# A fused layer in fp32 halves: the inverse's masks moved from GpSimd to the products' way out of PSUM, the first MLP products in source order, and the last stores issued behind the next loads

## The chip, the cores and the metric

One core of a Trainium2 chip runs the whole program. The metric is the device time of one execution in microseconds, median of several runs. Engines are named as in the profile: PE (TensorE matmul), PEld (its weight loads), DVE (VectorE), ACT (ScalarE), POOL (GpSimd), and SP, whose queue issues all the DMAs of this kernel.

## The reference, cut to what matters

One layer on x of 1024 tokens x 1024 channels (DEPTH is 1):

```python
u = rms_norm(h, norm_mix); proj = u @ w_in                      # 1024 x 2568
pool_out = pool_mixer(proj[:, :512], w_pool, pool_scale)        # 4 groups, trailing means of 2, 4, 8, 16 frames
qkv = causal_conv_silu(proj[:, 512:2048], conv_w)
gdn_out = gated_delta_net(q, k, v, z, a, b, ...)                # 4 heads of 128; solves (I + M) X = R, M strictly lower
h = h + concat(pool_out, gdn_out) @ w_out
u = rms_norm(h, norm_mlp)
h = h + square(relu(u @ w_up)) @ w_down                         # w_up 1024 x 4096, w_down 4096 x 1024
out = rms_norm(h, norm_final)
```

The kernel takes the delta rule in chunks of 128 tokens. In each chunk and head it needs the inverse of a unit lower triangular 128 x 128 matrix.

## The kernel before, in words

Every large product is made of three fp32r matmuls: an operand is split into a rounded part ("hi", a cast by ACT) and the rest ("lo", a subtraction by DVE or POOL), and hi x hi, hi x lo and lo x hi are added up in one PSUM bank (`mm3`).

**Order of the work.** PE's order is written out by hand: the whole program stands in `tc.manual_schedule(engines={PE})`, and in the first half a virtual clock (`T.now`) interleaves the dense projections with eight strands of small work. The other engines and SP are ordered by the planner of the framework, which plays the program through with its own costs. The planner also gives tiles their slots. `issue_after(ins)` puts what follows behind `ins` in the queue of its engine.

**Projection and delta rule (about 60 to 480 us of the span).** Dense projections run with `prepare`, `query`, `invert`, `correct` and `scan` between them, once for each of 8 chunks, for 4 heads at a time (tiles of 128 x 512). `invert` doubles the size of the inverted blocks seven times. Level 0 masks the matrix `m1` with `lev[0]` on DVE (L578) and adds the identity (L579). In each of the levels 1 to 6, POOL makes `bl = m1 * lev[l]` (L588), PE makes `px = bl^T t`, DVE takes it out of PSUM as `xx = px + ident` (L592), and PE makes the two products of the next level. The seven masks are made once on POOL at the start (L255 to L260: two memsets and two selects each). POOL also has the subtractions of `split_w` (L133) for half of the projections, and smaller steps.

**MLP, up (about 515 to 843 us).** One step of Strassen's scheme with seven products: `w_up` is taken in 16 pairs of 128-column blocks (`wu`, 1 MB each), and product i of pair p is 4 x 3 matmuls with the token operand `TH[i], TL[i]`. Pairs 0 and 1 run side by side in the order 1, 2, 6, 5, 3, 7, 4, because the operands for the second half of the tokens are made only now: `turn_second` transposes the normed tokens into 8 banks, makes the rows R11, R12, R2 from the banks (L908, L925) and splits operands 6 and 3; `operands_5`, `operands_7`, `operands_4` make the others (`parts_of`: L912 on ACT, L913 on DVE); `operands_7` also makes R4 = R21 - R2 on DVE (L943). `up_ready` prepares a weight operand: sums within `wu` (L970, L972, L975, L982; on DVE for pairs 0 and 1, on POOL for the others) and a split (L954 ACT, L955 DVE). `get_ready` runs `up_ready` two products ahead. `norm_v(1, 1)` norms the last two token tiles.

**MLP, down (from about 846 us).** Hidden values go through DRAM (`hd`): `keep` stores them at once (L994), but those of the last pair, but for product 1, are put on the list `late`. `down_load` fetches a block of `w_down` (L1103) and one of hidden values (L1106), four steps ahead, and the list `late` is stored after the first four. The pools of these tiles (`wr`, `xr`, `nf`, opened in this order) lie on the memory of the up stage's operands, tile by tile (`reuse_waits="tile"`): a load starts when the up operand under its slot has had its last matmul.

Of the kernel before, what the change touches and what calls it, by code (L numbers as in the profile page):

```python
# [8 lines left out]
F32 = mybir.dt.float32  # L9
F32R = mybir.dt.float32r  # L10
# [18 lines left out]
def hybrid_trunk(ctx, tc, x, norm_mix, w_in, conv_w, w_pool, pool_scale, a_log, dt_bias,  # L29
# [218 lines left out]

    lev = []
    for l in range(7):  # L250
        b = 1 << l
        m = gp.tile([P, P], F16, name=f"lev{l}")
        nb = P // (2 * b)
        m3 = m.rearrange("p (n q) -> p n q", q=2 * b)
        G.memset(m3[:, :, 0:b], 0.0)  # L255
        G.memset(m3[:, :, b:2 * b], -1.0)

        G.affine_select(m3, m3, pattern=[[-2 * b, nb], [0, 2 * b]], compare_op=ALU.is_ge, fill=0.0, base=0,
                        channel_multiplier=1)
        G.affine_select(m3, m3, pattern=[[2 * b, nb], [0, 2 * b]], compare_op=ALU.is_gt, fill=0.0, base=b,  # L260
                        channel_multiplier=-1)
        lev.append(m)
# [310 lines left out]
    def invert(c, r):  # L573

        m1 = r["m1"]
        t, tt = gt("t", 3, F16), gt("tt", 3, F16)
        b0 = gt("bl", 2, F16)
        V.tensor_tensor(b0, m1, bc(lev[0]), op=ALU.mult)  # L578
        V.tensor_tensor(tt, b0, bc(ident_h), op=ALU.add)  # L579
        yield 1.0 * SLACK  # L580
        pt = bank()
        for h in range(NH):
            T.matmul(pt[:, h, :], tt[:, h, :], ident_h, start=True, stop=True)
        A.copy(t, pt)
        yield 0.9 * SLACK
        for l in range(1, 7):
            bl = gt("bl", 2, F16)
            G.tensor_tensor(bl, m1, bc(lev[l]), op=ALU.mult)  # L588
            px = bank()
            mm(px, bl, t)  # L590
            xx = gt("xx", dt=F16)
            V.tensor_tensor(xx, px, bc(ident), op=ALU.add)  # L592
            yield 1.0 * SLACK
            pt, ptt = bank(), bank()
            mm(pt, tt, xx)
            mm(ptt, xx, tt)
            t, tt = gt("t", 3, F16), gt("tt", 3, F16)
            A.copy(t, pt)
            A.copy(tt, ptt)
            if l < 6:  # L600
                yield 1.0 * SLACK
        r.update(t=t, tt=tt)
        done(f"inverted{c}", 1.0 * SLACK)
# [279 lines left out]
    ys += norm_v(1, 1)  # L883
# [5 lines left out]
    R[12], R[2] = (u3(f"r{n}", F32) for n in (12, 2))  # L889
    TH[3], TL[3], TH[6], TL[6] = (u3(nm, F32R) for nm in ("th3", "tl3", "th6", "tl6"))  # L890

# [26 lines left out]
    def turn_second(ys):  # L918

        for k in range(KT):  # L920
            pt = turned_banks[k] = acc_bank() if k in (0, 1, 6, 7) else work_bank()
            turn(ys, k, pt)
            j = k % 4
            if k < 4:
                A.activation(R[12][:, j, :], pt, AF.Copy, scale=nmlp[:, k:k + 1])  # L925
                weighed(R[11][:, j, :], k, R[11][:, j, :])
            else:
                weighed(R[2][:, j, :], k, R[11][:, j, :])
        parts_of(6, rows_of(2))
        for j in range(4):  # L930
            weigh(turned_banks[4 + j], 4 + j, TH[3][:, j, :], TL[3][:, j, :], nmlp)

    def operands_5():
        TH[5], TL[5] = (big_tile(f"t{m}5", [4, HALF], F32R) for m in "hl")
        parts_of(5, rows_of(11))

    def operands_7():

        for j in range(4):
            weighed(R[12][:, j, :], 4 + j, R[12][:, j, :])  # L940
        R[4] = [c_tile("r4") for _ in range(4)]
        for j in range(4):
            V.tensor_tensor(R[4][j], R[21][:, j, :], R[2][:, j, :], op=ALU.subtract)  # L943
        TH[7], TL[7] = u3("th7", F32R), big_tile("tl7", [4, HALF], F32R)
        parts_of(7, rows_of(12))
# [17 lines left out]

    def up_ready(p, i):
# [3 lines left out]
        eng = V if p < 2 else G  # L968
# [7 lines left out]
        if i == 1 and p < 2:  # L976
            out = split(src, [P, 4, P], cp, "c", "c", 9)
        else:
            out = split(src, [P, 4, P], ws, "wh", "wl", 5)
        made2.add((p, i))  # L980
        if i in (2, 6) and {(p, 2), (p, 6)} <= made2:
            eng.tensor_tensor(a12, a12, a11, op=ALU.subtract)  # L982
        return out

    late = []

# [27 lines left out]
    def up_product(p, i, w):  # L1014
# [27 lines left out]
        else:  # L1042
# [5 lines left out]
    order = [(0, 1), (1, 1), lambda: turn_second(ys), (0, 2), (1, 2), operands_5, (0, 6), (1, 6), operands_7,  # L1048
             (0, 5), (1, 5), (0, 3), (1, 3), operands_4, (0, 7), (1, 7), (0, 4), (1, 4)]
# [20 lines left out]
    used = 0  # L1070
    for e in order:
        if callable(e):
            e()
            continue
# [8 lines left out]

    wrc, wr = opened(name="wr", bufs=4, side="right", reuse_waits="tile")
    xrc, xr = opened(name="xr", bufs=4, side="right", reuse_waits="tile")
    nfc, nf = opened(name="nf", bufs=1, side="right", reuse_waits="tile")
# [8 lines left out]
    def down_load(i, s):  # L1095
# [10 lines left out]
        nc.sync.dma_start(out=x, in_=hd[s][i])  # L1106
# [61 lines left out]
    for n, (i, s) in enumerate(todo):  # L1168
# [3 lines left out]
        while late:  # L1172
            store(*late.pop(0))
# [16 lines left out]
    close(spc)  # L1190
    close(nfc)
    close(xrc)
    close(wrc)
# [30 lines left out]
```

## Time and profile before

| | us |
|---|---|
| runs (3): median, lowest, highest | 1162.3, 1160.35, 1165.93 |
| the profiled execution: its own time | 1163.48 |
| its span | 1161.8 |
| PE busy | 1100.9 |
| DVE busy | 789.8 |
| ACT busy | 601.5 |
| POOL busy | 303.5 |

The profiled execution is 1.2 us above the median of the runs, and its span leaves 1.7 us of its own time outside. The granted clock of PE was 0.987 of full speed over the span. PE is "busy" also while it runs at half clock, so its busy time is not all work at full speed.

### The profile page before, as it was taken

What the parts mean: (1) busy time and instruction counts of PE and PEld (TensorE: products, weight loads), DVE (VectorE), ACT (ScalarE), POOL (GpSimd) and SP (SyncE); (2) the same over time, 40 slices, a digit from 0 to 9 for tenths busy, and PEclk for the clock granted to TensorE, in tenths of its full rate; (3) what the DMA queues carried; (4) which work ended last, traced back from release to release, by engine and by line L of the source; (5) the groups of instructions that cost most, each with busy time, mean ns of one, the idle gap of its engine ahead of it and who ended that gap; (6) DMA issues with size and microseconds to landing.
All of it is one profiled execution on the core that took longest, in us unless ns stands there. A gap on an engine that the chain in (4) does not pass through costs nothing.

```text
span 1161.8 us, 15593 instructions
## 1 busy us (share of the span) xinstructions
PE 1100.9 (95%) x5606; PEld 893.6 (77%) x5606; DVE 789.8 (68%) x1240; ACT 601.5 (52%) x1113; POOL 303.5 (26%) x272
## 2 busy tenths in 40 slices
PE   6998999988998999997999999999989999999997
PEld 5776777767776787876788888888878888888886
DVE  5798688867879775669655555555465687466584
ACT  6666566564755555546554544454444334335353
POOL 6033365564755422000232313131100000000010
PEclk9999999998999999998999999999989999999999
DMA  5233121111223321120634343444298796265561
GB/s 161 82 98 121 56 59 41 55 52 40 55 60 118 109 65 55 37 73 18 209 133 166 128 162 137 156 144 146 89 373 298 270 393 224 94 199 194 186 215 73
DMA packets 93049, 155.24 MB, mean 134 GB/s; under 512 B 7782, under 2 KB 45739, under 8 KB 92971
## 3 DMA queue, kind: packets, MB, share of 16 engines
q1 hardware_dynamic: 92970, 154.24, 39.4%
q8 instruction: 44, 0.72, 0.3%
q14 instruction: 35, 0.28, 0.1%
HBM read 120.66 MB, written 33.55 MB: 133 GB/s over the span
## 4 chain that ended last, share of the span: by engine, by line
PE 70%; DVE 13%; ACT 3%; issue 2%; POOL 1%; DMA 1%; POOLq 0%; DVEq 0%; ACTq 0%
PE bank L44 52%; PE acc L44 18%; DVE cy L391 2%; DVE nxt L410 1%; DVE xx L592 1%; PE bank L48 1%; DVE wl L955 1%; DVE nxt L409 0%; DMA wu<-in_w_up_dram 0%; DVE r L908 0%; DVE tl L913 0%; ACT th L172 0%; DVE ul L173 0%; DMA raw<-in_w_out_dram 0%; DVE kn L533 0%
## 5 line engine op out<-in xcount | busy, mean ns | idle before, releaser
L44 PE MATMUL bank<-tl,wh 128*128 128x512 f32 x440 | 175.3, 398 | 5.8 <-DVE tl L913 5.8
L44 PE MATMUL bank<-th,wh 128*128 128x512 f32 x440 | 175.2, 398 | 0.3 <-ACT p L1024 0.3
L44 PE MATMUL bank<-th,wl 128*128 128x512 f32 x440 | 174.7, 397 | 0.0
L954 ACT CAST sh<-x 128x1024 fp32r<-128x1024 f32 x55 | 57.9, 1053 | 163.8 <-PE bank L44 155.1
L954 ACT CAST wh<-wu 128x512 fp32r<-128x512 f32 x110 | 68.0, 620 | 127.2 <-PE bank L44 120.7
L44 PE MATMUL bank<-th,sh 128*128 128x512 f32 x344 | 133.8, 389 | 0.0
L44 PE MATMUL bank<-th,sl 128*128 128x512 f32 x344 | 133.8, 389 | 0.0
L44 PE MATMUL bank<-tl,sh 128*128 128x512 f32 x344 | 133.8, 389 | 0.0
L44 PE MATMUL acc<-uh,wh 128*128 128x512 f32 x320 | 130.3, 407 | 1.6 <-DVE ul L173 0.9
L44 PE MATMUL acc<-ul,wh 128*128 128x512 f32 x320 | 129.3, 404 | 0.0
L44 PE MATMUL acc<-uh,wl 128*128 128x512 f32 x320 | 128.9, 403 | 0.0
L955 DVE TENSOR_TENSOR sl<-x,sh 128x1024 fp32r<-128x1024 f32 x55 | 67.3, 1224 | 89.5 <-ACT sh L954 89.4
L44 PEld LDWEIGHTS bank<-tl,wh 128*128 128x128 f32 x440 | 83.5, 190 | 26.8 <-DVE tl L913 7.8
L955 DVE TENSOR_TENSOR wl<-wu,wh 128x512 fp32r<-128x512 f32 x110 | 84.4, 768 | 28.4 <-ACT wh L954 26.8
L44 PEld LDWEIGHTS bank<-th,wh 128*128 128x128 f32 x440 | 83.3, 189 | 20.1 <-ACT p L1024 0.8
L44 PEld LDWEIGHTS bank<-th,wl 128*128 128x128 f32 x440 | 83.5, 190 | 19.3
L152 POOL TENSOR_TENSOR stf<-stf,mhalf 128x1 f32<-128x1 f32 x8 | 7.9, 998 | 327.3 <-DVE stf L1159 327.3
L588 POOL TENSOR_TENSOR bl<-m,lev 128x512 f16<-128x512 f16 x48 | 62.9, 1310 | 84.7 <-PE bank L44 72.3
L391 DVE SCALAR_TENSOR_TENSOR cy<-cr,cols,cy 128x512 f32<-128x512 f32 x72 | 73.2, 1022 | 9.0 <-ACT cy L389 8.4
L133 POOL TENSOR_TENSOR wl<-raw,wh 128x512 fp32r<-128x512 f32 x48 | 68.0, 1420 | 35.6 <-ACT wh L132 35.4
L44 PEld LDWEIGHTS bank<-th,sl 128*128 128x128 f32 x344 | 64.6, 188 | 13.5
L44 PEld LDWEIGHTS bank<-th,sh 128*128 128x128 f32 x344 | 64.5, 188 | 13.5
(336 smaller groups left out, 2365.4 us busy)
## 6 DMA issues: line engine op xcount, KB each, us to landing
w<-in_w_down_dram SPq DMA_DIRECT2D x72, 512.0 KB, 5.9
x<-hd SPq DMA_DIRECT2D x56, 512.0 KB, 3.5
raw<-in_w_in_dram SPq DMA_DIRECT2D x80, 256.0 KB, 2.7
wu<-in_w_up_dram SPq DMA_DIRECT2D x16, 1024.0 KB, 5.3
hd<-s SPq DMA_DIRECT2D x48, 256.0 KB, 2.3
raw<-in_w_out_dram SPq DMA_DIRECT2D x24, 256.0 KB, 2.7
xin<-in_x_dram SPq DMA_DIRECT2D x8, 512.0 KB, 5.3
h<-in_x_dram SPq DMA_DIRECT2D x8, 512.0 KB, 4.4
```

The lines of the kernel that those rows point to most:

```text
L44: T0.matmul(out, lhsT, rhs, start=start, stop=stop, skip_group_check=goes_on)
L48: T0.transpose(out, in_, identity)
L133: eng.tensor_tensor(lo, raw, hi.bitcast(F32), op=ALU.subtract)
L152: last["rsqrt"] = G.tensor_tensor(s, s, mhalf[:, :n], op=ALU.pow)
L391: V.scalar_tensor_tensor(cy, cr[:, e:e + HALF], tap[e], cy, op0=ALU.mult, op1=ALU.add)
L410: V.tensor_tensor(nxt[:, n:], cur[:, n:], cur[:, :W - n], op=ALU.add)
L588: G.tensor_tensor(bl, m1, bc(lev[l]), op=ALU.mult)
L592: V.tensor_tensor(xx, px, bc(ident), op=ALU.add)
L954: A.copy(hi, src)
L955: V.tensor_tensor(lo, src, hi.bitcast(F32), op=ALU.subtract)
```

## The change

Three parts. (1) `invert` multiplies with the full `m1` and puts the mask on the product as DVE takes it out of PSUM: `xx = px * lev[l]`, with masks that are turned round and have ones on the diagonal; POOL's 48 masking steps go, and level 0 is one DVE step in place of two. The masks take one select more each. (2) For the first 14 up products PE, DVE and ACT run in source order; operand 5 is made ahead of 6 and its product goes ahead; R4 and two of the weight sums move from DVE to POOL; the first block of `w_up` of pairs 0 and 1 gets loads of its own (`first_load`, 256 KB each) ahead of `norm_v(1, 1)`. (3) The late stores are issued behind the last of the first loads of the down stage, and the pools are opened in another order (`nf`, `xr`, `wr`).

```diff
@@ masks
-        G.memset(m3[:, :, 0:b], 0.0)
-        G.memset(m3[:, :, b:2 * b], -1.0)
...
+        first = l > 0
+        G.memset(m3[:, :, 0:b], -1.0 if first else 0.0)
+        G.memset(m3[:, :, b:2 * b], 0.0 if first else -1.0)
...
+        G.affine_select(m, m, pattern=[[-1, P]], compare_op=ALU.not_equal, fill=1.0, base=0, channel_multiplier=1)
@@ invert
-        b0 = gt("bl", 2, F16)
-        V.tensor_tensor(b0, m1, bc(lev[0]), op=ALU.mult)
-        V.tensor_tensor(tt, b0, bc(ident_h), op=ALU.add)
+        V.tensor_tensor(tt, m1, bc(lev[0]), op=ALU.mult)
...
-            bl = gt("bl", 2, F16)
-            G.tensor_tensor(bl, m1, bc(lev[l]), op=ALU.mult)
             px = bank()
-            mm(px, bl, t)
+            mm(px, m1, t)
             xx = gt("xx", dt=F16)
-            V.tensor_tensor(xx, px, bc(ident), op=ALU.add)
+            V.tensor_tensor(xx, px, bc(lev[l]), op=ALU.mult)
@@ operands of the up products
-    ys += norm_v(1, 1)
...
-    R[12], R[2] = (u3(f"r{n}", F32) for n in (12, 2))
     TH[3], TL[3], TH[6], TL[6] = (u3(nm, F32R) for nm in ("th3", "tl3", "th6", "tl6"))
+    R[2], R[12] = (u3(f"r{n}", F32) for n in (2, 12))
...
     def turn_second(ys):
+        TH[5], TL[5] = (big_tile(f"t{m}5", [4, HALF], F32R) for m in "hl")
         for k in range(KT):
             pt = turned_banks[k] = acc_bank() if k in (0, 1, 6, 7) else work_bank()
             turn(ys, k, pt)
...
+        for k in range(4):
+            A.activation(R[12][:, k, :], turned_banks[k], AF.Copy, scale=nmlp[:, k:k + 1])
+            weighed(R[11][:, k, :], k, R[11][:, k, :])
+        parts_of(5, rows_of(11))
+        for j in range(4):
+            weighed(R[2][:, j, :], 4 + j, R[11][:, j, :])
         parts_of(6, rows_of(2))
+
+    def operands_3():
+        R[4] = [c_tile("r4") for _ in range(4)]
         for j in range(4):
+            G.tensor_tensor(R[4][j], R[21][:, j, :], R[2][:, j, :], op=ALU.subtract)
             weigh(turned_banks[4 + j], 4 + j, TH[3][:, j, :], TL[3][:, j, :], nmlp)
...
     def operands_7():
...
-        R[4] = [c_tile("r4") for _ in range(4)]
-        for j in range(4):
-            V.tensor_tensor(R[4][j], R[21][:, j, :], R[2][:, j, :], op=ALU.subtract)
@@ weights of the up products
+    def first_load(p):
+        r = ws.tile([P, 4, P], F32, name="raw", tag="raw", bufs=3)
+        nc.sync.dma_start(out=r, in_=wuv[:, :4, p * 256:p * 256 + P])
+        return split(r, [P, 4, P], cp, "c", "c", 9)
...
-        eng = V if p < 2 else G
+        eng = V if p < 2 and i in (1, 6) else G
...
         if i == 1 and p < 2:
-            out = split(src, [P, 4, P], cp, "c", "c", 9)
+            out = first_parts[p]
...
+        eng = G
         if i in (2, 6) and {(p, 2), (p, 6)} <= made2:
             eng.tensor_tensor(a12, a12, a11, op=ALU.subtract)
...
+    first_parts = [first_load(p) for p in range(2)]
+    ys += norm_v(1, 1)
@@ order
-    order = [(0, 1), (1, 1), lambda: turn_second(ys), (0, 2), (1, 2), operands_5, (0, 6), (1, 6), operands_7,
-             (0, 5), (1, 5), (0, 3), (1, 3), operands_4, (0, 7), (1, 7), (0, 4), (1, 4)]
+    order = [(0, 1), (1, 1), lambda: turn_second(ys), (0, 2), (1, 2), operands_3, (0, 5), (1, 5), operands_7, (0, 6), (1, 6),
+             (0, 3), (1, 3), operands_4, (0, 7), (1, 7), (0, 4), (1, 4)]
+    N_FIRST = 14
...
+        if e == (0, 1):
+            get_ready(3)
+            in_order.enter_context(tc.manual_schedule(engines={mybir.EngineType.PE, mybir.EngineType.DVE, mybir.EngineType.Activation}))
+        elif used == N_FIRST:
+            in_order.close()
         if callable(e):
+            get_ready(used + 2 + LEAD)
             e()
@@ down
+    nfc, nf = opened(name="nf", bufs=1, side="right", reuse_waits="tile")
+    xrc, xr = opened(name="xr", bufs=4, side="right", reuse_waits="tile")
     wrc, wr = opened(name="wr", bufs=4, side="right", reuse_waits="tile")
-    xrc, xr = opened(name="xr", bufs=4, side="right", reuse_waits="tile")
-    nfc, nf = opened(name="nf", bufs=1, side="right", reuse_waits="tile")
...
-        nc.sync.dma_start(out=x, in_=hd[s][i])
+        last["load"] = nc.sync.dma_start(out=x, in_=hd[s][i])
...
-        while late:
-            store(*late.pop(0))
+        if late:
+            with tc.issue_after(last["load"].ins):
+                while late:
+                    store(*late.pop(0))
```

## Rows read from the trace of the kernel before

**Rows 1.** The page's busy time, share of the span and count of each engine.
```profile
PE 1100.9 (95%) x5606; PEld 893.6 (77%) x5606; DVE 789.8 (68%) x1240; ACT 601.5 (52%) x1113; POOL 303.5 (26%) x272
```

**Rows 2.** Busy time by stage. Columns: the stretch, its length, busy time (and count) of PE, PEld, DVE, ACT, POOL, then PE's mean granted clock, the DMA share and GB/s.
```profile
60.00:480.00 420.00, 390.34 (x2503) 316.95 (x2502) 326.37 (x607) 246.53 (x568) 197.64 (x151) 0.98 0.22 67
...
515.00:560.00 45.00, 37.20 (x163) 28.55 (x162) 40.59 (x66) 26.06 (x48) 1.34 (x2) 0.92 0.14 48
560.00:840.00 280.00, 279.67 (x1203) 226.48 (x1202) 158.29 (x230) 139.09 (x230) 72.72 (x56) 1.00 0.41 145
840.00:860.00 20.00, 16.76 (x61) 12.81 (x60) 13.72 (x16) 10.86 (x14) 0.00 (x0) 0.83 0.97 341
```

**Rows 3.** What PE waited for from 60 to 480 us: us in total, times, the longest.
```profile
PE bank L44 <- DVE xx L592: 15.3, 10, 3.0
PE bank L48 <- DVE kn L533: 2.9, 2, 1.5
```

**Rows 4.** What PE waited for from 440 us to the end, same columns.
```profile
PE bank L44 <- DVE tl L913: 5.8, 3, 5.3
PE bank L44 <- ACT wh L954: 3.2, 1, 3.2
PE bank L44 <- DVE c L955: 1.7, 2, 1.5
```

**Rows 5.** POOL's groups over the whole span: count, then busy us and mean ns of one, then idle time before them and its releasers.
```profile
L588 POOL TENSOR_TENSOR bl<-m,lev 128x512 f16<-128x512 f16 x48 | 62.9, 1310 | 84.7 <-PE bank L44 72.3 <-DVE tt L579 7.2 <-DVE m L550 3.6
...
L258 POOL TENSOR_SCALAR_AFFINE_SELECT lev<-lev 128x128 f16<-128x128 f16 x7 | 2.9, 416 | 0.0
```

**Rows 6.** DVE's groups from 60 to 440 us, same columns.
```profile
L391 DVE SCALAR_TENSOR_TENSOR cy<-cr,cols,cy 128x512 f32<-128x512 f32 x56 | 60.0, 1076 | 7.5 <-ACT cy L389 7.0
L592 DVE TENSOR_TENSOR xx<-bank,ident 128x512 f16<-128x512 f32 x45 | 30.7, 683 | 14.5 <-PE bank L44 14.4
...
L764 DVE TENSOR_TENSOR ml<-pT,mh 128x512 fp32r<-128x512 f32 x8 | 8.4, 1058 | 0.0
L393 DVE SCALAR_TENSOR_TENSOR vT<-vT,cy 128x512 f32<-128x512 f32 x8 | 8.0, 995 | 1.8 <-ACT vT L392 1.8
...
L578 DVE TENSOR_TENSOR bl<-m,lev 128x512 f16<-128x512 f16 x8 | 6.5, 809 | 0.1
...
L619 DVE TENSOR_TENSOR hh<-bank,tt 128x512 f16<-128x512 f32 x7 | 4.8, 681 | 0.2 <-PE bank L44 0.2
```

**Rows 7.** Durations of single lines, ns min/median/max: the convolution's taps from 60 to 440 us, `xx` and the split of `pT` over the span.
```profile
L391 DVE SCALAR_TENSOR_TENSOR cy<-cr,cols,cy x56: 736/752/1833, 59.8 to 315.8; 128x512 f32<-128x512 f32 x56
...
L592 DVE TENSOR_TENSOR xx<-bank,ident x48: 671/682/693, 89.1 to 452.7; 128x512 f16<-128x512 f32 x48
...
L764 DVE TENSOR_TENSOR ml<-pT,mh x16: 678/682/1777, 369.0 to 504.8; 128x512 fp32r<-128x512 f32 x16
```

**Rows 8.** PE's instructions in order of time from 515 to 545 us: start, us, engine, line, operation, out<-in, count, and in brackets the idle time before.
```profile
522.81 1.04 PE L48 MATMUL acc<-ident,xn 128*128 128x128 f32 x8
...
526.95 0.48 PE L44 MATMUL bank<-th,wh 128*128 128x512 f32 x1
527.26 0.39 PE L44 MATMUL bank<-tl,wh 128*128 128x512 f32 x1
527.49 0.40 PE L44 MATMUL bank<-th,wl 128*128 128x512 f32 x1
...
540.34 0.80 PE L44 MATMUL bank<-tl,wh 128*128 128x512 f32 x1 [5.27 <-DVE tl L913]
540.93 0.63 PE L44 MATMUL bank<-th,wl 128*128 128x512 f32 x1
541.36 0.63 PE L44 MATMUL bank<-th,wh 128*128 128x512 f32 x1
```

**Rows 9.** DVE in the same stretch, in order of time, same columns.
```profile
526.40 2.72 DVE L908 SCALAR_TENSOR_TENSOR r<-bank,cols,r 128x512 f32<-128x512 f32 x4
...
537.19 2.49 DVE L943 TENSOR_TENSOR r<-r,r 128x512 f32<-128x512 f32 x4
```

**Rows 10.** Durations of single lines from 500 to 575 us, ns min/median/max: the splits of `wu` on DVE, and a weight sum on POOL.
```profile
L955 DVE TENSOR_TENSOR wl<-wu,wh x18: 679/683/1283, 515.8 to 574.5; 128x512 fp32r<-128x512 f32 x18
...
L970 POOL TENSOR_TENSOR wu<-wu x2: 1296/1300/1304, 559.5 to 562.8; 128x512 f32<-128x512 f32 x2
```

**Rows 11.** SP's issues around 840 us in order of time.
```profile
839.81 0.32 SPq L994 DMA_DIRECT2D hd<-v  x1
840.22 0.39 SPq L1103 DMA_DIRECT2D w<-in_w_down_dram  x1
840.66 0.50 SPq L1106 DMA_DIRECT2D x<-hd  x1
843.35 0.38 SPq L1103 DMA_DIRECT2D w<-in_w_down_dram  x1
```

**Rows 12.** ACT around 845 us in order of time.
```profile
844.75 0.63 ACT L998 ACTIVATE p<-p 128x512 f32<-128x512 f32 x1
845.35 0.62 ACT L954 CAST wh<-x 128x512 fp32r<-128x512 f32 x1
```

**Rows 13.** PE from 842 to 853 us in order of time.
```profile
846.54 0.79 PE L44 MATMUL bank<-wh 128*128 128x512 f32 x1 [3.22 <-ACT wh L954]
...
852.22 0.48 PE L44 MATMUL bank<-wh 128*128 128x512 f32 x1
```

More of the change, by code (lines that the diff above doesn't have):

```diff
@@ L254, in hybrid_trunk @@
         m3 = m.rearrange("p (n q) -> p n q", q=2 * b)
-        G.memset(m3[:, :, 0:b], 0.0)
-        G.memset(m3[:, :, b:2 * b], -1.0)
-        G.affine_select(m3, m3, pattern=[[-2 * b, nb], [0, 2 * b]], compare_op=ALU.is_ge, fill=0.0, base=0,
+        first = l > 0
+        G.memset(m3[:, :, 0:b], -1.0 if first else 0.0)
+        G.memset(m3[:, :, b:2 * b], 0.0 if first else -1.0)
+        o = b if first else 0
+        G.affine_select(m3, m3, pattern=[[-2 * b, nb], [0, 2 * b]], compare_op=ALU.is_ge, fill=0.0, base=-o,
                         channel_multiplier=1)
-        G.affine_select(m3, m3, pattern=[[2 * b, nb], [0, 2 * b]], compare_op=ALU.is_gt, fill=0.0, base=b,
+        G.affine_select(m3, m3, pattern=[[2 * b, nb], [0, 2 * b]], compare_op=ALU.is_gt, fill=0.0, base=o + b,
                         channel_multiplier=-1)
+        G.affine_select(m, m, pattern=[[-1, P]], compare_op=ALU.not_equal, fill=1.0, base=0, channel_multiplier=1)
         lev.append(m)
@@ L922, in turn_second @@
             turn(ys, k, pt)
[L923 to L928, printed above, removed]
+        for k in range(4):
[4 more added lines that the diff above has]
+            weighed(R[2][:, j, :], 4 + j, R[11][:, j, :])
         parts_of(6, rows_of(2))
+    def operands_3():
+        R[4] = [c_tile("r4") for _ in range(4)]
         for j in range(4):
+            G.tensor_tensor(R[4][j], R[21][:, j, :], R[2][:, j, :], op=ALU.subtract)
             weigh(turned_banks[4 + j], 4 + j, TH[3][:, j, :], TL[3][:, j, :], nmlp)
-    def operands_5():
-        TH[5], TL[5] = (big_tile(f"t{m}5", [4, HALF], F32R) for m in "hl")
-        parts_of(5, rows_of(11))
     def operands_7():
@@ L1070, in hybrid_trunk @@
     used = 0
+    in_order = ExitStack()
     for e in order:
+        if e == (0, 1):
[3 more added lines that the diff above has]
+            in_order.close()
         if callable(e):
+            get_ready(used + 2 + LEAD)
             e()
@@ L1190, in hybrid_trunk @@
     close(spc)
+    close(wrc)
+    close(xrc)
     close(nfc)
-    close(xrc)
-    close(wrc)
     close(psgc)
```

## Prediction

> **What bounds the kernel now.** I read the busy table first: PE works 95% of the span, the next engine 68% [rows 1]. So time is won where PE waits or runs slow, and nowhere else. The table by stage says where that is [rows 2]. From 560 to 840 us PE idles 0.3 us of 280; nothing is to be had there. From 60 to 480 us it idles 29.7 us of 420 with the clock at 0.98, which is another 8.4 us of full speed lost, 38 in all. From 515 to 560 it idles 7.8 us at a clock of 0.92, from 840 to 860 3.2 us at 0.83. The waits then say for whom: in the long stage mostly for DVE's `xx`, 15.3 us in ten waits [rows 3], in the two short ones for DVE's splits, 5.8 and 1.7 us, and for one ACT cast, 3.2 us [rows 4].
>
> **Part 1, masks.** POOL loses 48 steps, 62.9 us [rows 5]. PE never waits for them by name: `bl` is early, POOL itself waited 72.3 us for PE to free its two buffers. So the direct gain is nothing; the indirect one is DVE. The taps of the convolution take 752 ns in the median but 1833 at most and 1076 in the mean of 56, while `xx`, with one input in PSUM, lies between 671 and 693 always [rows 6, 7]. What stretches DVE's steps is POOL's work beside them, so I take the excess over the median as the price of POOL: 56 x (1076 - 752) = 18.1 us for the taps, 8 x (1058 - 682) = 3.0 for the split of `pT`, 8 x (995 - 752) = 1.9 for `vT` (nearest row: the taps), 23 us in these alone [rows 6, 7]. `bl` is 62.9 of POOL's 197.6 us in the stage, 32% [rows 2, 5], so some 7 us of this go, and the eight level-0 masks with them, 6.5 us [rows 6]. DVE then works 313 us of 420 in place of 326: 74.5% in place of 77.7%.
>
> The Trainium skill (SBUF — State Buffer, section "Who interferes with whom") gives the mechanism: a VectorE instruction with two SBUF inputs contends with a GpSimd instruction that reads SBUF, the first to start holds the shared ports for its whole length, and an instruction with at most one SBUF input is not touched. The trace agrees on both sides (taps up to 1833 ns, `xx` never over 693 [rows 7]). That rule speaks against part 2, which moves steps to POOL; rival 5 is that case, priced from rows.
>
> What that does to PE I can only estimate. PE waits because DVE has a queue in front of `xx`, and a queue grows as u/(1 - u) with the busy share u: 3.49 before, 2.92 after, 16% less. POOL's own results (`kn` waits for its power, 2.9 us [rows 3]) come earlier as well, so I take a fifth of the 38 us: **-7.6 us**. The new `xx` costs nothing: a product of a PSUM bank with an fp16 tile is nearest to `hh`, a bank plus an fp16 tile in 681 ns, against 683 now [rows 6]; PE's products keep their shapes. Against it stand seven more selects at the start, 7 x 0.416 = 2.9 us of POOL beside the first weights [rows 5]; between nothing (they fill POOL's waits) and 2.9 I take **+0.5**. Bounds of the part: +2.9, if the queue stays as it is, and -18.2 for all the waits of [rows 3]; with the clock's 8.4 us -26.6.
>
> **Part 2, first up products.** The losses from 515 to 560 us are 7.8 us of idle time [rows 2] and a slow stretch behind the longest wait: matmuls start 0.43 us apart at 541 in place of 0.23, the clock at its lower level, for ten of them by the timeline, 2.0 us [rows 8]. The first 1.7 us are a wait for operand `c`, whose split stood behind other work on DVE [rows 4]; its load of its own comes before, DVE has free time then, so 1.7 goes. The longest, 5.27 us, is a wait for a split of operand 6, while DVE did R4 (2.49 us) and parts of operands 3 and 7 first [rows 8, 9].
>
> I walk through the new order. Transposes start 1.7 us earlier than 522.81, at 521.1, product 2 at about 525.0 [rows 8]. DVE's four R11 (2.72 us) and four splits of operand 5 (2.49) [rows 9] start with the first bank at some 521.6 and end at 526.8. PE wants operand 5 after two products of 12 x 0.23 = 2.76 us, at 530.5: 3.7 us spare. Four R2 and four splits of operand 6 end at 532.0, wanted at 536.0: spare 4.0. After that DVE has 23 steps up to product 7 (two weight sums, five weight splits, four splits of operand 3, four of R12, four splits of operand 7, four additions of products 5 and 6), at about 0.63 each, and two round trips over ACT of 0.6: 15.7 us, so 547.7, where PE wants them at 530.5 + 6 x 2.76 = 547.1: 0.6 late. POOL now runs eight steps of 1.30 us here (R4 four times, four weight sums), and a split beside POOL took 1.28 us in place of 0.68 [rows 10], so 8 x 0.6 = 4.8 us are added if every one of them hits a step of DVE, 5.4 late. I take 1.8: half of these DVE steps read PSUM, and POOL need not hit each time. Part 2: -7.8 - 2.0 + 1.8 = **-8.0**, between -9.8 and -4.4. A harder price is rival 5.
>
> Other queues of this part: on SP the two new loads stand ahead of `wu`, 0.5 MB in a stretch with the queue idle. In ACT's source order the cast for pair 2 waits for its `wu`, which leaves when pair 0's last split is through; it lands before PE wants it by my count, with 1 to 2 us spare, because PE now arrives there 8 us earlier.
>
> **Part 3, start of the down stage.** PE waits 3.22 us, and then 12 matmuls take from 846.54 to 852.22, 5.7 us in place of 2.8, with the clock at its lower level [rows 13]: 6.1 us lost. Two things stand in front of PE. On SP the first load of weights left at 840.22 right behind a late store at 839.81, the second only at 843.35, with the end of the last up product, because its slot lies on operand 4 [rows 11]. On ACT the first cast of the down stage, at 845.35, stands right behind the square of the last product, 844.75 to 845.38 [rows 12]. In the new order of the pools `nf` lies on operand 4 and the `w` slots on operand 1, which is free early; the first slot reaches 256 bytes into the up stage's next pool, most likely on operand 7, whose last matmul ends two products of 2.76 us before 843.35. Loads can then leave at about 837.8, 2.4 us earlier, and the planner can put the cast before the square: PE's wait shrinks to some 0.5 us and the slow stretch goes, -5.6. If the planner leaves the cast behind the square, nothing is won. Nearer to the first: **-3.8**. The late stores cost nothing behind the loads: all but the one of 839.81 stand there already, and no wait of PE in the down stage is longer than this one.
>
> **The sum:** -7.6 + 0.5 - 8.0 - 3.8 = -18.9. The profiled execution took 1163.5, so 1144.6; it lay 1.2 above the median, so I say **1144 us**.
>
> **Rivals.**
> 1. *The masks give nothing.* PE never waited for `bl`, and its order is written by hand; DVE's queue may be as long at the places where PE looks. Then 1163.5 + 0.5 - 8.0 - 3.8 = 1152. Chance 0.18 alone.
> 2. *The masks give much more.* If DVE's shorter queue closes most waits, the slow clock behind the longest ones goes too: -18 in place of -7.6, 1134. Chance 0.11.
> 3. *The loads change nothing* (part 3 does not do what it says): the `w` slot's 256 bytes lie under an operand of the last two products, and the first load leaves at 840.5 or later. Then 1144.6 + 3.8 = 1148, inside the forecast's own range; chance 0.15, some half of it with rival 1, which is 1156.
> 4. *Slower: the planner's new order.* It re-plans DVE, ACT and SP over 420 us with costs that no longer hold POOL's steps. It already put R4 ahead of a split that PE wanted: 5.27 + 2.0 = 7.3 us [rows 8]. Parts 2 and 3 give 11.3; one such place more in the long stage leaves a gain, two are +3.3 and 1167, three are +10.6 and 1174. From two on the kernel is no longer faster, from three on it is slower by more than runs can hide. For it: the planner knows no stretching by POOL. Against it: with POOL emptier its plan is nearer to the chip. Chance 0.05.
> 5. *POOL holds DVE.* Each of POOL's eight new steps beside the first up products holds a DVE step for its whole 1.30 us: product 7 comes 0.6 + 10.4 = 11.0 us late, part 2 is -9.8 + 11.0 = +1.2, the time 1154. For it: taps of the long stage reach 1833 ns, 1.08 over their median [rows 7]. Against it: the split beside POOL lost 0.6 [rows 10], and DVE's steps on PSUM nothing. Chance 0.04.
>
> **Chances and range.** Forecast (1140 to 1150, with rival 3 alone) 0.54, rival 1 0.18, rivals 1 and 3 together 0.08, rival 2 0.11, rival 4 0.05, rival 5 0.04. I count 0.5% (6 us) as what a measurement of this kernel can tell from no change; the line is 1156.5. Faster: 0.54 + 0.18 + 0.11 + 0.04 = 0.87. Rivals 1 and 3 together lie at the line, so same 0.08; slower 0.05. The range from 1136 to 1155 leaves out rival 4, half of rival 2 and rivals 1 and 3 together, 0.19.
>
> **What would show it.** Part 1: no L588, taps with a lower mean than 1076, waits for `xx` under 15.3 us, idle time from 60 to 480 near 24 us. Part 2: no wait over 2 us for a split between 515 and 560, product 5 ahead of 6 without a gap, a short one at product 7. Part 3: the first loads of the down stage leave before the last product's matmuls start, PE's wait there under 1 us and full clock behind it. I am wrong if the long stage's idle time stays or grows, or if DVE, now bound to source order, keeps PE waiting at product 7 for over 5 us.

## The result: the forecast time was nearly met, by parts that were all of another size

| | before | after |
|---|---|---|
| median of 4 runs each, us | 1162.55 | 1148.64 |
| profiled span, us | 1161.8 | 1145.7 |
| ratio, 95% interval | | 0.9877 [0.9852, 0.9901] |

The changed kernel is 13.9 us faster. The forecast was 1144 us, its range 1136 to 1155. But the experiments put part 1 at -17.7 us (forecast -7.1), part 2 at +2.4 (forecast -8.0) and part 3 at nothing (forecast -3.8). Errors of opposite sign cancel, so that the total fell into the range is luck.

The page's busy table after, against [rows 1]. POOL lost 47 us, DVE 28, PE 4.

```profile
PE 1096.5 (96%) x5606; PEld 891.3 (78%) x5606; DVE 761.5 (66%) x1224; ACT 599.8 (52%) x1113; POOL 256.2 (22%) x239
```

The table by stage after, columns as in [rows 2]. The second stretch runs from the first up product to the end of the first 14.

```profile
60.00:480.00 420.00, 402.61 (x2597) 328.07 (x2596) 313.09 (x621) 262.07 (x597) 135.54 (x104) 0.99 0.23 71
...
495.69:554.05 58.36, 48.68 (x201) 37.33 (x200) 44.87 (x64) 31.77 (x56) 16.24 (x12) 0.91 0.17 54
```

In the stretch from 60 to 480 us PE idles 17.4 us in place of 29.7 (the prediction looked for some 24), at a clock of 0.99 in place of 0.98. A fixed stretch holds more work in a faster kernel, though (2597 matmuls against 2503). From 60 us to the first up product the work is the same. Before, then after:

```profile
60.00:515.01 455.01, 423.80 (x2664) 344.15 (x2663) 347.32 (x641) 268.24 (x607) 200.56 (x155) 0.98 0.23 69
60.00:495.69 435.69, 418.30 (x2665) 340.83 (x2664) 320.19 (x633) 268.24 (x608) 137.17 (x107) 0.99 0.24 73
```

For the same matmuls PE idles 17.4 us in place of 31.2, and DVE works 27 us less, twice what the forecast had. The waits from 60 to 480 us, against [rows 3], and DVE's groups from 60 to 440 us, against [rows 6]:

```profile
PE bank L44 <- DVE xx L595: 3.4, 7, 0.8
```

```profile
L396 DVE SCALAR_TENSOR_TENSOR cy<-cr,cols,cy 128x512 f32<-128x512 f32 x56 | 51.1, 914 | 4.1 <-ACT cy L394 3.6
L595 DVE TENSOR_TENSOR xx<-bank,lev 128x512 f16<-128x512 f32 x48 | 32.9, 685 | 16.3 <-PE bank L44 16.1
```

The taps fell from 1076 to 914 ns in the mean, `xx` kept its duration (683, now 685), and the waits for it went from 15.3 to 3.4 us. The first 14 up products, however, take 58.4 us, where the kernel before needs 53.8 for as many matmuls:

```profile
515.01:568.80 53.79, 45.99 (x201) 35.66 (x200) 47.69 (x74) 31.36 (x56) 6.71 (x6) 0.94 0.19 64
```

Idle time went from 7.8 to 9.7 us, busy time from 46.0 to 48.7. PE's main waits there in the changed kernel, in order of time (the bracket is the wait), against [rows 8]:

```profile
497.84 0.74 PE L44 MATMUL bank<-th,c 128*128 128x512 f32 x2 [1.53 <-DVE c L955]
...
520.01 0.50 PE L44 MATMUL bank<-th,wh 128*128 128x512 f32 x1 [1.37 <-ACT wh L954]
...
521.26 0.80 PE L44 MATMUL bank<-th,wl 128*128 128x512 f32 x1 [0.52 <-DVE wl L955]
...
534.70 0.47 PE L44 MATMUL bank<-th,wh 128*128 128x512 f32 x1 [1.02 <-DVE u L1040]
...
545.83 0.77 PE L44 MATMUL bank<-th,wh 128*128 128x512 f32 x1 [4.27 <-DVE v L1045]
```

The wait of 5.27 us is gone, but the one for `c` (1.53) stayed and one of 4.27 us is new, with shorter ones between. Behind 520.01 and 545.83 matmuls start 0.43 us apart in place of 0.23, 6 and 13 of them: 19 x 0.2 = 3.8 us, against 6 such matmuls in the kernel before (the prediction counts ten). DVE in the same stretch says why, against [rows 9]; the last two lines are the splits of operand 6 and R4 on POOL one by one (ns min/median/max, first and last start):

```profile
513.23 5.47 DVE L915 TENSOR_TENSOR tl<-r,th 128x512 fp32r<-128x512 f32 x4
518.62 0.68 DVE L978 TENSOR_TENSOR wu<-wu 128x512 f32<-128x512 f32 x1
519.99 1.22 DVE L955 TENSOR_TENSOR wl<-wu,wh 128x512 fp32r<-128x512 f32 x1 [0.68 <-ACT wh L954]
...
541.38 1.29 DVE L955 TENSOR_TENSOR wl<-wu,wh 128x512 fp32r<-128x512 f32 x2 [1.87 <-ACT wh L954]
542.59 2.49 DVE L915 TENSOR_TENSOR tl<-r,th 128x512 fp32r<-128x512 f32 x4
545.00 1.28 DVE L1045 TENSOR_TENSOR v<-bank,v 128x512 f32<-128x512 f32 x2
...
L915 DVE TENSOR_TENSOR tl<-r,th x4: 680/1612/1799, 513.2 to 518.0; 128x512 fp32r<-128x512 f32 x4
...
L937 POOL TENSOR_TENSOR r<-r,r x4: 1319/1542/1767, 511.5 to 515.8; 128x512 f32<-128x512 f32 x4
```

The four splits of operand 6 took 5.47 us in place of 2.49. Three ran beside R4 on POOL and took up to 1.80 us each; the fourth, from 518.0, behind the end of R4, took 0.68. And the addition of product 7's bank (L1045), which PE needs before it may put product 4 into the same bank, stands in DVE's source order behind two weight splits that wait for ACT and four splits of operand 4. At the down stage ACT and PE, against [rows 12, 13]:

```profile
829.39 0.63 ACT L1007 ACTIVATE p<-p 128x512 f32<-128x512 f32 x1
829.93 0.60 ACT L954 CAST wh<-x 128x512 fp32r<-128x512 f32 x1
```

```profile
831.10 0.50 PE L44 MATMUL bank<-wh 128*128 128x512 f32 x1 [3.13 <-ACT wh L954]
832.01 0.79 PE L44 MATMUL bank<-wl,wh 128*128 128x512 f32 x1 [0.40 <-DVE wl L955]
```

SP issues the first two loads at 822.40 and 822.84, over 5 us ahead of the up stage's end, as forecast; but the cast still stands behind the square, and PE waits 3.13 us as before (3.22).

### The profile page after: what moved, and what is told of

It is laid out like the page before. It is cut to its first block, busy times and chain, and to the rows that moved or that the text cites. A ratio compares the mean times of both kernels' runs of the same rounds, so it can differ in the third digit from the quotient of the medians.

```text
span 1145.7 us, 15530 instructions
## 1 busy us (share of the span) xinstructions
PE 1096.5 (96%) x5606; PEld 891.3 (78%) x5606; DVE 761.5 (66%) x1224; ACT 599.8 (52%) x1113; POOL 256.2 (22%) x239
## 4 chain that ended last, share of the span: by engine, by line
PE 73%; DVE 10%; ACT 3%; POOL 2%; issue 2%; POOLq 0%; DVEq 0%
PE bank L44 54%; PE acc L44 18%; DVE cy L396 2%; DVE tl L915 1%; PE bank L48 1%; DVE wl L955 1%; DVE r L910 1%; POOL rk L152 1%; DVE xx L595 0%; ACT th L172 0%; POOL wl L133 0%; DVE nxt L415 0%; DVE m L551 0%; DVE nxt L414 0%; ACT wh L954 0%
## 5 line engine op out<-in xcount | busy, mean ns | idle before, releaser
L44 PEld LDWEIGHTS bank<-tl,sh 128*128 128x128 f32 x344 | 64.6, 188 | 13.5
L44 PEld LDWEIGHTS acc<-uh,wh 128*128 128x128 f32 x320 | 60.3, 188 | 13.4 <-ACT cy L394 1.6
```

The costliest lines, as they stand in the source:

```text
L44: T0.matmul(out, lhsT, rhs, start=start, stop=stop, skip_group_check=goes_on)
```

## The experiments

The runs were made in three sets, each beside runs of the kernel before on its own chip: 1162.6, 1165.1 and 1164.4 us. Across sets only ratios are compared; 0.001 is 1.16 us. One stretch can be compared in microseconds: from the start of the first up product to that of the first down product. It holds parts 2 and 3 and nothing of part 1. Each figure of it is one profiled execution: before, masks, pool_busy and pool_memset have the same instructions there and lie from 331.5 to 332.8, so I read nothing into a difference of some 1.3 us or less.

| kernel | contains | ratio, 95% | first up | first down | between |
|---|---|---|---|---|---|
| before | | 1 | 515.01 | 846.54 | 331.5 |
| after | parts 1, 2, 3 | 0.9877 [0.9852, 0.9901] | 495.69 | 831.10 | 335.4 |
| masks | part 1 | 0.985 [0.983, 0.9871] | 496.53 | 829.35 | 332.8 |
| pool_busy | part 1, 48 products left on POOL | 0.9991 [0.9979, 1.0003] | 512.78 | 845.09 | 332.3 |
| pool_memset | part 1, 144 memsets on POOL | 0.9848 [0.9833, 0.9862] | 496.98 | 829.23 | 332.3 |
| mlp | part 2 | 1.0027 [1.0012, 1.0042] | 513.33 | 848.95 | 335.6 |
| stores | part 3 | 1.0006 [0.999, 1.0023] | 513.76 | 846.10 | 332.3 |
| op4_early | after, operands 4 earlier | 0.9851 [0.9837, 0.9866] | 495.95 | 831.16 | 335.2 |
| casts_first | op4_early, down casts first | 0.9834 [0.9818, 0.9851] | 496.12 | 828.92 | 332.8 |
| no_mlp_casts | parts 1 and 3, down casts first | 0.9799 [0.9784, 0.9813] | 496.83 | 825.89 | 329.1 |
| planned | casts_first, DVE and ACT by the planner | 0.9782 [0.9756, 0.9809] | 495.50 | 823.58 | 328.1 |
| late_hidden | casts_first, squares later | 0.9863 [0.984, 0.9885] | 495.90 | 832.02 | 336.1 |
| r4_after_6 | no_mlp_casts, R4 later | 0.9788 [0.9764, 0.9811] | 494.81 | 823.02 | 328.2 |
| five_first | no_mlp_casts, product 5 ahead of 6 | 0.9746 [0.9719, 0.9772] | 495.71 | 818.94 | 323.2 |

### Each part alone

`masks` is the change's masks and `invert`, `mlp` its operands, weights and order of the up products, `stores` its part for the down stage; each leaves the rest as before.

> Part 1 alone on the kernel before. If the traces' landmark is right (the first up product starts at 495.7 us after and at 515.0 before), part 1 is worth 19 us: 1143 us, and the waits for xx fall from 15.3 to some 3.5 us. If the forecast's size was right and the rest comes from elsewhere: 1155 us.

> Part 2 alone. By the landmarks the 14 first up products take 58.4 us from the first matmul to the last in place of 53.8: 4.6 us slower, 1167 us, with a wait of some 4 us ahead of product 4 for DVE's addition to product 7's bank and half clock behind it. Rival: the loss is there only because part 1 brings other work beside it; then the forecast's 8 us gain shows, 1154 us.

> Part 3 alone. By the traces the loads leave 2.5 us earlier against the end of the up stage, but ACT's first cast still stands behind the last square: 0 to 1 us faster, 1161.5 to 1162.5 us, with the wait of PE near 3.2 us. The forecast's size would be 1158.7 us.

Measured medians: masks 1144.86 us, mlp 1164.99, stores 1162.75, beside 1162.56 of the kernel before. Part 1 alone gains 17.7 us, more than the whole change. Part 2 costs 2.4 us, part 3 changes nothing. The sum, -15.1, is within 1.2 us of what the whole does, so the parts hardly act on one another. In masks the waits for `xx` are 2.8 us in place of 15.3. PE's longest waits of mlp and of the down stage of stores are those of after again, at other times:

```profile
563.48 0.47 PE L44 MATMUL bank<-th,wh 128*128 128x512 f32 x1 [4.28 <-DVE v L1042]
```

```profile
846.10 0.49 PE L44 MATMUL bank<-wh 128*128 128x512 f32 x1 [3.13 <-ACT wh L954]
```

### What of part 1 gives the time: POOL, or the shorter chain?

Part 1 takes 48 steps from POOL, eight level-0 steps from DVE, and one step out of the chain of `invert`. `pool_busy` keeps the new chain and gives POOL its 48 products back; nobody uses what they make.

```diff
@@ masks -> pool_busy, in each level 1 to 6
+            bl = gt("bl", 2, F16)
+            G.tensor_tensor(bl, t, bc(lev[l]), op=ALU.mult)
```

> Part 1, but POOL still does 48 multiplications of 128x512 in fp16, one in each level, whose results nobody reads. Theory A (POOL's work beside DVE stretches DVE's steps, and this is what the masks free): the gain goes, 1156 to 1162 us, taps of the convolution near 1076 ns again. Theory B (it is the order: the planner no longer plans the product behind POOL's step, so it puts xx where PE wants it): the gain stays, 1143 to 1147 us, though the taps are stretched again.

Measured: 1161.54 us, nothing left of the gain but some 1 us. From 60 us to the first up product, masks and then pool_busy, and pool_busy's wait for `xx` and its taps:

```profile
60.00:496.53 436.53, 419.90 (x2664) 341.91 (x2663) 319.34 (x633) 267.97 (x607) 136.63 (x107) 0.99 0.24 72
60.00:512.78 452.78, 424.07 (x2665) 344.21 (x2664) 342.37 (x633) 268.05 (x607) 201.25 (x155) 0.98 0.23 69
```

```profile
PE bank L44 <- DVE xx L597: 11.9, 10, 4.3
```

```profile
L396 DVE SCALAR_TENSOR_TENSOR cy<-cr,cols,cy 128x512 f32<-128x512 f32 x56 | 58.5, 1046 | 4.7 <-ACT cy L394 4.2
```

The same 633 steps of DVE take 23 us more, and PE idles 28.7 us in place of 16.6; all is nearly as in the kernel before (31.2 us idle, 15.3 us of waits for `xx`, taps of 1076 ns). So it is POOL's work that costs PE the time, not the chain. But it could be that POOL is busy (its other results come late, or the planner plans otherwise), or that it takes something from DVE. `pool_memset` makes POOL as busy with steps that read nothing:

```diff
@@ masks -> pool_memset
-        t, tt = gt("t", 3, F16), gt("tt", 3, F16)
+        t, tt = gt("t", 4, F16), gt("tt", 3, F16)
...
             mm(px, m1, t)
+            for _ in range(3):
+                G.memset(t, 0.0)
```

> Part 1 alone, with 144 memsets on POOL (three of 128x512 fp16 in each of the levels 1 to 6, written over the matrix that PE has just read, which gets a fourth buffer): POOL is as busy as in the kernel before (some 60 to 75 us more than with part 1 alone), but reads no SBUF in these steps. Theory A1 (DVE's steps with two SBUF inputs are stretched by POOL's reads): taps stay at a mean near 923 ns, the time stays at 1145 to 1148. Theory A2 (any step of POOL beside DVE stretches it, or the planner's order changes with POOL's load): taps at a mean near 1046 ns and 1158 to 1162 us, as with the 48 unused products. Between 1149 and 1157: both.

Measured: ratio 0.9848, that of masks. The same work, its memsets and its taps:

```profile
60.00:496.98 436.98, 419.42 (x2666) 341.44 (x2664) 321.83 (x633) 267.47 (x607) 203.87 (x251) 0.99 0.24 72
```

```profile
L595 POOL MEMSET t<- 128x512 f16 x144 | 76.3, 532 | 93.7 <-PE bank L44 65.6 <-ACT junk L510 12.2 <-ACT pT L438 6.2
```

```profile
L396 DVE SCALAR_TENSOR_TENSOR cy<-cr,cols,cy 128x512 f32<-128x512 f32 x56 | 52.6, 942 | 7.7 <-ACT cy L394 7.2
```

POOL is busy for 203.87 us, more than in the kernel before (200.56), and PE loses next to nothing by it: it idles 17.6 us, 0.9 more than in masks, and DVE works 2.5 us more. Here a busy POOL is harmless, and a POOL that reads two operands is not. The Trainium skill (SBUF — State Buffer, section "Who interferes with whom") says it so: a VectorE instruction with two SBUF inputs contends with a GpSimd instruction that reads SBUF, not with one that only writes it. These two runs agree with it: 62.7 us of reading steps undo the gain, 76.3 us of writing steps cost nothing. One reserve: the two kernels differ also in that the memsets are three short steps, and that `t` has a fourth buffer there, while in pool_busy POOL's read holds one of three. A held buffer could make PE wait; it would not lengthen DVE's steps, and those are 23 us longer.

### Part 2: where its loss sits

`op4_early` moves one entry of the order of the changed kernel:

```diff
@@ after -> op4_early
-             (0, 3), (1, 3), operands_4, (0, 7), (1, 7), (0, 4), (1, 4)]
+             operands_4, (0, 3), (1, 3), (0, 7), (1, 7), (0, 4), (1, 4)]
```

> All three parts, with the operands of product 4 made ahead of product 3 instead of behind it. Theory A (the loss of part 2 sits at product 4: its first matmul waits 4.27 us for DVE's addition of product 7's bank, because four splits that wait for ACT's casts stand ahead of it in DVE's source order, and 13 matmuls at half clock follow, 2.6 us): the wait is under 0.5 us, no stretch at half clock behind it, and the time is 1148.6 - 6.9 = 1141.7 us. Theory B (ACT and DVE are full in this stage, and source order merely moves the wait): a wait of 3 us or more turns up at another product (3 or 7), time 1146 to 1149.

Measured: 335.2 us between the marks, as after (335.4). Theory A falls: the wait at product 4 went from 4.27 to 2.65 us and the half clock behind it from 13 to 7 matmuls, but 0.66 and 0.40 us turned up at product 3 and 1.82 behind the 14 products. Theory B's single wait of 3 us did not come either; the loss is spread. What stands ahead of the addition now, ACT first, then DVE:

```profile
539.66 0.63 ACT L1006 ACTIVATE u<-u 128x512 f32<-128x512 f32 x1 [4.07 <-DVE u L1049]
540.32 0.63 ACT L1007 ACTIVATE u<-u 128x512 f32<-128x512 f32 x1
540.86 0.61 ACT L1006 ACTIVATE u<-u 128x512 f32<-128x512 f32 x1
541.50 0.63 ACT L1007 ACTIVATE u<-u 128x512 f32<-128x512 f32 x1
542.04 0.60 ACT L954 CAST wh<-wu 128x512 fp32r<-128x512 f32 x1
```

```profile
542.67 0.69 DVE L955 TENSOR_TENSOR wl<-wu,wh 128x512 fp32r<-128x512 f32 x1 [2.45 <-ACT wh L954]
543.28 0.68 DVE L1045 TENSOR_TENSOR v<-bank,v 128x512 f32<-128x512 f32 x1
```

ACT waited 4.07 us for DVE's addition, did four steps of squares and only then the cast; DVE waited 2.45 us for that cast, with the addition that PE wanted behind it. In source order the two engines wait for each other by turns. `planned` gives DVE and ACT back to the planner, on top of casts_first (below):

```diff
@@ casts_first -> planned
-            in_order.enter_context(tc.manual_schedule(engines={mybir.EngineType.PE, mybir.EngineType.DVE, mybir.EngineType.Activation}))
```

> casts_first, with DVE and ACT put in order by the planner again for the first 14 up products, and nothing else changed; PE's order, R4 and the two weight sums on POOL and product 5 ahead of 6 stay. Theory A (the loss of part 2 comes from the source order: DVE's splits stand behind ACT's squares, and ACT's casts behind DVE's additions): the time from the first up product to the first down product falls from 332.8 us to 328 or less, and the whole is 0.4% or more under casts_first, some 1139 us where the kernel before has 1162.5. Theory B (R4 on POOL holds DVE's splits of operand 6, and the planner knows nothing of it): no change against casts_first, 332 us and 1143.7.

Measured: 328.1 us between the marks in place of 332.8, at the bound of Theory A (328 or less), and a ratio 0.0052 lower. The source order costs 4.7 us. What PE still waits for in planned, and DVE ahead of it:

```profile
521.02 0.80 PE L44 MATMUL bank<-tl,wh 128*128 128x512 f32 x1 [3.98 <-DVE tl L915]
```

```profile
512.37 2.39 DVE L915 TENSOR_TENSOR tl<-r,th 128x512 fp32r<-128x512 f32 x2
...
515.35 2.39 DVE L915 TENSOR_TENSOR tl<-r,th 128x512 fp32r<-128x512 f32 x2
```

Splits beside R4 on POOL took 1.2 us each in place of 0.6, so POOL's price is paid in the planner's order too. `late_hidden` tried to mend the source order itself:

```diff
@@ casts_first -> late_hidden: the squares of products 7 and 3, and the squares and additions of 4, run behind the next product
-            hidden(m["v5"], m["v5"])
-            keep(p, 4, m["v5"])
+            after_next(p, seven)
```

> casts_first, and within the source order of the first 14 up products the squares and the combinations of a product are put behind the preparation of the next weights and the next product's own addition. Theory A (source order puts ACT's casts behind four steps of squares): the wait of 2.65 us at product 4, the 2 us of half clock behind it and the 1.9 us behind the 14 products go, but for some 0.7; 327 to 328 us from the first up to the first down product, 1138 to 1139 where the kernel before has 1162.5. Theory B (DVE itself is full there): 331 us or more, 1142 or more.

Measured: 336.1 us, 3.3 worse than casts_first. That lies within the bound of Theory B, but not for its reason: DVE was not full (busy 45.65 of the 58.10 us from 495.90 to 554.00). The wait at product 4 fell to 1.47 us, but pair 2 now starts late:

```profile
560.88 0.79 PE L44 MATMUL bank<-th,wh 128*128 128x512 f32 x1 [4.80 <-ACT p L1046]
```

```profile
558.69 1.66 ACT L954 CAST wh<-wu 128x512 fp32r<-128x512 f32 x3 [3.30 <-POOL wu L981]
560.25 0.57 ACT L1046 COPY p<-bank 128x512 f32<-128x512 f32 x1
```

ACT stands at a cast that waits for POOL's weight sum, with the copy that frees PE's bank behind it: the same fault at another place.

### The down stage: the cast ahead of the square

`casts_first` and `no_mlp_casts` issue the last product's squares and additions behind the first cast and split of the down stage.

```diff
@@ op4_early -> casts_first, after the first loads of the down stage
+        if n == 0:
+            ready[todo[0]] = down_ready(*todo[0])
+            n_made = 1
+            with tc.issue_after(last["cast"].ins), tc.issue_after(last["sub"].ins):
+                ending.pop()()
```

> op4_early, and at the start of the down stage the last product's squares and additions are issued behind the first cast (ACT) and the first split (DVE) of the down stage. Theory A (part 3 won nothing because the first cast of the down stage still stands behind the square of the last product on ACT, 829.93 behind 829.39): PE's wait of 3.13 us there falls to some 1 us, the split's 0.40 us go, the matmuls behind run at full clock, and the time is 3 to 4 us under op4_early, 1138. Theory B (the loads are the limit): the wait stays at 2.5 us or more, no change against op4_early.

> Parts 1 and 3 without part 2, and with the first cast and split of the down stage ahead of the last squares. If part 2 costs 2.4 us as it did alone, part 3 gives nothing alone and the casts 3 to 4 us: 1144.9 - 3.5 = 1141.4 us, 3 us over casts_first. If part 3's loads matter only once the cast is free: the same. If the cast ahead of the squares gives nothing: 1144.9.

Measured: 2.4 us less between the marks than op4_early and 1.7 in the medians of the same set (1146.22, 1147.88), less than the 3 to 4 us expected. no_mlp_casts has 0.9799 and lies under casts_first, not 3 us over it: I had counted on op4_early to heal part 2. Under masks it lies by 3.7 us between the marks and by 0.005 of the ratio, some 6 us, but across sets; part of it is a shorter stretch at half clock behind operand 6 (3 matmuls in place of 10, behind the same wait). PE of casts_first:

```profile
828.92 0.50 PE L44 MATMUL bank<-wh 128*128 128x512 f32 x1 [0.62 <-ACT wh L954]
830.28 0.50 PE L44 MATMUL bank<-wl,wh 128*128 128x512 f32 x1 [0.85 <-DVE wl L955]
```

The wait is 0.62 us and the matmuls behind it run 0.23 us apart, but DVE's splits now cost 0.85 and 0.24. So the square ahead of the cast was the last thing that PE waited for. Whether part 3 is needed for this gain was not run: in casts_first the cast waits for the hidden values until 827.73, 4.6 us after their load was issued, and 4.6 us after the load of the kernel before [rows 11] would be 845.3, just where its cast stood [rows 12].

### Product 5 ahead of 6, without the rest of part 2

Both start from no_mlp_casts, which keeps the old 5.27 us wait at operand 6.

```diff
@@ no_mlp_casts -> five_first
-    order = [(0, 1), (1, 1), lambda: turn_second(ys), (0, 2), (1, 2), operands_5, (0, 6), (1, 6), operands_7,
-             (0, 5), (1, 5), (0, 3), (1, 3), operands_4, (0, 7), (1, 7), (0, 4), (1, 4)]
+    order = [(0, 1), (1, 1), lambda: turn_second(ys), (0, 2), (1, 2), operands_5, (0, 5), (1, 5), operands_7,
+             (0, 6), (1, 6), (0, 3), (1, 3), operands_4, (0, 7), (1, 7), (0, 4), (1, 4)]
@@ no_mlp_casts -> r4_after_6
-        for j in range(4):
-            V.tensor_tensor(R[4][j], R[21][:, j, :], R[2][:, j, :], op=ALU.subtract)
+        with tc.issue_after(last["six"].ins):
+            for j in range(4):
+                V.tensor_tensor(R[4][j], R[21][:, j, :], R[2][:, j, :], op=ALU.subtract)
```

> no_mlp_casts, with product 5 ahead of product 6 for pairs 0 and 1, and nothing else of part 2. DVE split operand 5 ahead of operand 6 there anyway, and PE waited 5.27 us for operand 6 and ran 2 us of lost time at half clock behind it. If the order of the products is what the planner's order wants: this wait falls under 1 us, 329.1 - 6 = 323 us from the first up to the first down product and 1133 us where the kernel before has 1162.5. If the planner turns its own order round with it: a wait of 3 to 5 us at product 5 or 7, 328 to 330 us and 1138 to 1140.

> no_mlp_casts, with the four steps of R4 on DVE issued behind the last split of operand 6, and nothing else. R4 (2.49 us) stood ahead of the split that PE waited 5.27 us for. If R4's place sets that wait: it falls to 2.8 us or less and the half clock behind it shortens, 325 to 327 us from the first up to the first down product, 1135 to 1137 us where the kernel before has 1162.5. If the other steps in front (R12, splits of operand 5) set it: 328 to 329 us, 1138 to 1139.5.

Measured: five_first 323.2 us between the marks, the 323 expected, and a ratio of 0.9746. PE does not wait for operand 6 at all; new are 1.39 us for a split of operand 7 and 1.47 at product 4. With 1134.97 us beside 1164.41 it beats both kernels, the changed one by 0.0131 of the ratio, some 15 us. r4_after_6 lies 0.9 us under no_mlp_casts there, the second of the two cases and no more than the figures scatter: its wait fell from 5.27 to 2.87 us, but 1.05 and 0.41 came up later and more matmuls ran at half clock (8 in place of 3 by the timeline); the ratios do not tell it from no_mlp_casts. PE of five_first, its longest waits:

```profile
530.88 0.50 PE L44 MATMUL bank<-tl,wh 128*128 128x512 f32 x1 [1.39 <-DVE tl L916]
...
538.88 0.47 PE L44 MATMUL bank<-th,wh 128*128 128x512 f32 x1 [1.47 <-DVE v L1039]
```

No matmul of that stretch started 0.43 us after the one before. The planner re-plans DVE with each of these edits, so a difference between two of them is the edit with its new plan. From five_first (323.2) to planned (328.1) the rest of part 2 comes in, above all R4 and weight sums on POOL and the other order of the helpers: 4.9 us, not separated further.

## Why the prediction was right, and where it was not

**Part 1: the mechanism right, two terms mis-sized.** The forecast saw that POOL stretches DVE, and that this reaches PE by the waits for `xx`.

The first term is POOL's price, 7 us of stretch ("32%" of three groups) and 6.5 for level 0, 13.5 in all. For the same work DVE gained 28.0 us in masks (347.3 to 319.3): 6.1 at level 0, 8.4 in the taps, and most of the rest in splits and small steps that the forecast did not price. DVE's 313 us of 420 came out by luck, because the fixed stretch holds more work now.

The second term is "a fifth of the 38 us". With the shares as measured (347.3 of 455.0 and 319.3 of 436.5 us) u/(1 - u) still falls by only 16%, and PE's idle time fell by 47% in masks (31.2 to 16.6). The same matmuls also took 3.9 us less at the higher clock (423.8 to 419.9): together 18.5 us, of which the waits for `xx` alone are 12.5. That formula treats DVE's queue as one at random; PE's order is fixed by hand, and it waits again and again at the same places. That this is why it gains more is my reading; no run separates it.

Rival 2 (-18) is what happened to this part; I gave it 0.11. The bounds of the part (+2.9 to -26.6) held it. The selects cost nothing visible: the first dense product of masks starts at 15.65 us, before at 15.52, and PE's busy time up to 60 us is 49.2 us against 49.1.

**Part 2: three steps failed, one held.** (a) "Its load of its own comes before, DVE has free time then, so 1.7 goes": 1.53 us of it stayed. The load was early and ACT had begun the cast of `c` at 492.65, but DVE stood idle for 1.40 us at the head of its queue, at L777, which waited for PE's bank, and did a weight split before `c`. An idle engine is not a free one when its queue is in order:

```profile
495.89 0.69 DVE L777 TENSOR_TENSOR h<-bank,h 128x512 f32<-128x512 f32 x1 [1.40 <-PE bank L44]
496.50 0.68 DVE L955 TENSOR_TENSOR wl<-wu,wh 128x512 fp32r<-128x512 f32 x1
497.10 1.29 DVE L955 TENSOR_TENSOR c<-raw,c 128x512 fp32r<-128x512 f32 x2
```

(b) "Spare 4.0" at product 6: POOL's R4 fell on the splits of operand 6 and made them 3.0 us longer; with the weight sums behind them PE waited 1.37 + 0.52 us. I had charged POOL's steps at product 7 alone, and 0.6 us for each; a split beside R4 lost up to 1.1 (1.80 against 0.68), which is rival 5's price, nearly a whole step of POOL. (c) At product 7 the size held, 1.02 + 0.40 where I had 1.8; the first of the two was for the addition that frees product 6's bank. (d) I stopped the walk there. Product 4 shares its bank with 7, and the source order puts the addition that frees it behind everything that stands earlier in the program: 4.27 us, and 13 x 0.2 = 2.6 at half clock. The warning sign I gave, over 5 us of waiting for DVE in source order, named the right cause one product too early. Rival 5 put part 2 at +1.2, by POOL; the runs show +2.4 in the medians and +4.1 between the marks (mlp against before). Between the marks the order of the products is worth -5.8 (five_first against no_mlp_casts), the source order +4.7 and the rest, R4 on POOL with it, +4.9.

**Part 3: the loads right, the planner wrong.** Loads leave over 5 us ahead of the stage's end, as worked out. "The planner can put the cast before the square" did not happen; by the forecast's own words nothing is then won. When the step is forced, casts_first gains 1.7 us in the medians and 2.4 between the marks, where I had up to 5.6: DVE's split comes next. Without part 2 the pair of masks and no_mlp_casts shows more (3.7 between the marks), so the size stays open.

Rival 3 named the time, 1148, by luck: part 3 gave nothing, but for another reason than rival 3's (the cast, not the loads), and parts 1 and 2 came out otherwise. A slip in the sum: 1144.6 less 1.2 is 1143.4, not 1144. Rival 4 did not come: the longest wait that is new in the long stage of masks is 1.5 us (for ACT's `qT`).

## What to carry to other kernels

Moving work off an engine that is never the last to be waited for can still be the largest gain, if that work reads memory beside the engine that is; price it by all of that engine's stretched steps, and then let the wait list, not an average load, say what the engine in front gets back. Compare stretches of the same work, not of the same length. When an engine is put into source order, walk every instruction up to the end of the ordered stretch, and for each wait name who stands behind it. Change the order of products and the order of helpers in two steps: here the first was worth 5.8 us (no_mlp_casts to five_first), and the rest of the part took 9.6 away (five_first 323.2, casts_first 332.8).

## What the runs showed of the hardware

- 144 memsets of 128x512 fp16 on POOL (532 ns each, 76.3 us) left the time at 0.9848 of before, 48 products of two fp16 operands (1305 ns each, 62.7 us) took it from 0.985 to 0.9991.
- Where POOL ran subtractions back to back (R4, up to 1.77 us each in place of 1.30), DVE's splits beside them took up to 1.80 us in place of 0.68: both engines are slowed, DVE to more than twice its time.
- The prediction says after the Trainium skill (SBUF — State Buffer, section "Who interferes with whom") that an instruction with at most one SBUF input is not touched. It leaves out the section's condition (outside the 2-port perf modes), and without it the rows speak against it: in the kernel before, copies of 128x3 with one input took 151 ns at least, 170 in the median and 1240 at most. This one ended as POOL's step beside it did, at 250.4 us; in which mode it ran no run shows:

```profile
248.65 1.74 POOL L756 TENSOR_TENSOR qT<-qT,zT 128x512 f32<-128x512 f32 x1
249.27 1.15 DVE L383 COPY cr<-chalo 128x3 f32<-128x3 f32 x1
```

- A wait of 1.37 us at 520.01 in the changed kernel was followed by six matmuls at the lower clock (0.43 us apart), one of 1.38 us at 520.27, at the same product in op4_early, by none, and neither was one of 1.39 us at 530.88 in five_first. Behind the same wait for operand 6 (5.29 and 5.27 us) masks has 10 such matmuls and no_mlp_casts 3. In op4_early the slow stretch began only with the matmul at 545.46, 1.35 us after PE had resumed at 544.11. Why, no run here shows.
